# Attention scores from stacked high and low halves of q and k, and two more weight blocks split on GpSimd, in a two-layer hybrid encoder

## The chip, the cores and the metric

One core of a Trainium2 chip runs the whole program. The metric is device time in microseconds (us). Below, PE is the matrix engine (TensorE), PEld its weight loads, DVE the VectorE, ACT the ScalarE, POOL the GpSimd, SP the engine whose queue issues the DMAs.

## What is computed

Two layers over 256 positions of width 1024, in float32. Each layer is a half SwiGLU feed-forward, a mixer and another half feed-forward, each followed by a residual and a LayerNorm. The mixer's three branches are fed by one projection; the attention branch is what the change touches:

```
z = x @ w_in
sc_b, sc_c, sc_h, q, k, v, cc_a, cc_gate = split(z)
y_sc = sc_b * dwconv3(sc_c * sc_h)
q, k = rope(q), rope(k)                       # 8 query heads, 2 key heads, 64 wide
y_att = softmax(q k^T / 8, |i-j| <= 128, learned sink per head) @ v
u = dwconv31(cc_a * sigmoid(cc_gate)) + cc_conv_b
y_cc = silu(layer_norm(u))
mixer = concat(y_sc, y_att, y_cc) @ w_out
```

## The kernel before

Weights come as blocks of 128x2048 float32 (1 MB), 78 per layer: 33 for a feed-forward, 12 for the mixer, 33 again. `fetch` (L102) has SP load a block into one of five `raw` buffers. `emit_block` (L115) splits it with `split` (L95): ACT rounds it to a float32r part `hi` (L96), and a subtraction gives the rest `lo` (L97). The subtraction is DVE's, in one piece of 128x2048, except for the blocks of `POOL_BLOCKS` (L43): these go to POOL in four pieces of 128x512. `ON_POOL` (L42) names them by their number from the mixer's first block, 7 to 15 before the change. `use` (L135) hands a split block to the matmuls, `release` and `tick` (L140, L147) emit the next split when a block has been read; five `hi` and `lo` buffers exist. Each float32 product is then three matmuls: hi*hi, hi*lo, lo*hi (`mm3`, L152).

`mixer` (L476) is written out by hand in its order, and a scheduler of the language then sets the order on each engine. First come the projections for the gate of the long convolution (`ga`) and for q (blocks 0 to 3, `proj_n`), then k and v (block 4, `kv`), then three column projections `proj_c` (block 5 into `psc`, 6 into `psh`, 7 into `psb`). `glu` and `glu_turned` make `upad`, the long convolution's padded input; `emit_conv` (L541) lays its 31 taps for two channel groups, 62 instructions of 128x256 that DVE does between other work (`fill`, L143; tap lines L549, L551). `rotate` applies the rotary embedding on DVE (L500 to L503).

`q_turned` and `k_turned` (L517, L524) transpose the rotated q and k on PE (L205) and have ACT copy them from PSUM (L521, L527). `scores` (L560) does, for a pair of heads in two groups j, plain float32 matmuls of 64 rows (L566): group j lives on partitions 64j to 64j+63 in both operands:

```
hp = slice(j * HD, (j + 1) * HD)
nc.tensor.matmul(scs[j][:, c, :], qT[t][hp, 2 * i + c, :], kT[hp, :], start=True, stop=False)
```

A bfloat16 matmul adds the mask (L568). There are eight such units, four in a layer: `S_(0)` to `S_(3)`. Each is followed by maxima on DVE (L576), exponentials on ACT, transposes (`T_`) and the product with v (`V_`). `cc_norm` and `cc_out` take the finished convolution through a LayerNorm and swish into `y[3]` (a pair yhh, yhl: rounded part and rest). `w_out` (L752) multiplies y[0] to y[3] by the output blocks, t being the tile of 128 positions and h the half of the columns. `boundary` (L281) closes the mixer: for tile 0 it gathers (L225), takes statistics (L220), normalises (L239, L240) and transposes the result for the next feed-forward.

Of the kernel before, what the change touches and what calls it, by code (L numbers as in the profile page):

```python
# [8 lines left out]
F32 = mybir.dt.float32  # L9
F32R = mybir.dt.float32r  # L10
BF16 = mybir.dt.bfloat16
AF = mybir.ActivationFunctionType
ALU = mybir.AluOpType
# [3 lines left out]
P = 128  # L17
D = 1024
S = 256
# [5 lines left out]
HD = 64  # L25
# [13 lines left out]
PER_MIX = 12  # L39
NBLOCKS = DEPTH * (2 * PER_FFN + PER_MIX)  # L40
W_OUT = (1, 2, 0, 3)
ON_POOL = range(7, 16)  # L42
POOL_BLOCKS = [l * (2 * PER_FFN + PER_MIX) + PER_FFN + i for l in range(DEPTH) for i in ON_POOL]  # L43


@with_exitstack
def encoder(ctx: ExitStack, tc: tile.TileContext, head_in, xt_in, x_in, w_in, gb_in, small_in, rope_in, out):
    nc = tc.nc
# [9 lines left out]
    mx = pool("mx", 1)  # L58
# [144 lines left out]
    def transpose(ps, srcs):  # L203
        for i, a in enumerate(srcs):
            nc.tensor.transpose(ps[:, i * P:(i + 1) * P], a, ident)  # L205
# [270 lines left out]
    def mixer(l, norm):  # L476
# [11 lines left out]
        nc.gpsimd.memset(upad, 0.0)  # L488
        ppad = mx.tile([P, 2, S + 2], F32, tag="ppad", name="ppad")
        nc.gpsimd.memset(ppad, 0.0)  # L490
        kT = mx.tile([P, S], F32, tag="kT", name="kT")
        half = HD // 2
        chan = lambda a: a.rearrange("p (c n) -> p c n", c=2)

# [19 lines left out]
            transpose(pt, [u[:, 0:P], u[:, P:2 * P]])  # L514
            nc.scalar.copy(upad[:, :, PAD + t * P:PAD + (t + 1) * P], chan(pt[:, 0:2 * P]))

        def q_turned(r):  # L517
            pq = tmp_bank()
            transpose(pq, [r[:, c * P:(c + 1) * P] for c in range(4)])
            q = mx.tile([P, 4, P], F32, tag="qT", bufs=2, name="qT")  # L520
            nc.scalar.copy(q.rearrange("p c n -> p (c n)"), pq)  # L521
            return q

        def k_turned(t, r):  # L524
            pk = tmp_bank()
            transpose(pk, [r[:, 0:P]])
            nc.scalar.copy(kT[:, t * P:(t + 1) * P], pk[:, 0:P])  # L527

        def kv(t, w):
            ps = tmp_bank()  # L530
# [29 lines left out]
        def scores(t, i):  # L560
            mo = 1 - t
            scs = [chan(bank()) for _ in range(2)]
            for c in range(2):
                for j in range(2):
                    hp = slice(j * HD, (j + 1) * HD)
                    nc.tensor.matmul(scs[j][:, c, :], qT[t][hp, 2 * i + c, :], kT[hp, :], start=True, stop=False)  # L566
                for j in range(2):
                    nc.tensor.matmul(scs[j][:, c, mo * P:(mo + 1) * P], ident_b, mask[:, t, :], start=False, stop=True)  # L568
            return scs

# [80 lines left out]
        qT, vn, rk = [], [], []  # L651
        ga, q = bank(), bank()
# [6 lines left out]
        r0 = rotate(0, q, NH)  # L659
# [2 lines left out]
        glu_turned(0, u0)  # L662
        proj_n(ga, 1, wga[1], 1)
        u1 = glu(ga)
        qT.append(q_turned(r0))
        proj_n(q, 1, wq[0], 0)
        glu_turned(1, u1)
        cacc = emit_conv()
# [10 lines left out]
        wc = use(KC)  # L679
        fill(6)  # L680
        proj_c(psc, wc, 0)
        qT.append(q_turned(r1))
        k_turned(0, rk0)
        k_turned(1, rk1)
        prs, pTs = {}, {}

        def softmax(u, scs):
# [196 lines left out]
```

## Time and profile before

| | |
|---|---|
| median of 3 runs | 935.88 us (935.44 to 935.91) |
| the profiled execution | 933.17 us, of which the span is 931.4 us |
| granted TensorE clock | 0.998 |
| PE busy | 918.5 us, 99% |
| DVE busy | 644.5 us, 69% |
| ACT busy | 458.5 us, 49% |
| POOL busy | 118.0 us, 13% |
| DMA | 174.01 MB, mean 187 GB/s |

The span runs from the first to the last instruction of the profiled execution; the other runs carry no trace. Busy shares are over the whole span; the two mixers lie at 189 to 279 us and at 648 to 738 us. In a timeline the starts of successive matmuls give what each one costs, as their shown durations overlap.

### The profile page before, as it was taken

The numbers are of one execution on the slowest core, as the hardware profiler recorded it, in microseconds if no ns is written. First come the engines' busy times: TensorE is split into PE (matmuls) and PEld (weight loads), VectorE is DVE, ScalarE is ACT, GpSimd is POOL, SyncE is SP. The second block draws the span as 40 slices with busy tenths as digits, with TensorE's granted clock in tenths as the row PEclk, the third lists the DMA queues.
The fourth block names the chain that finished last, engine by engine and source line by source line (L and its number), as shares of the span: only waits on it lengthen the run. The fifth ranks groups of instructions, "written<-read, shape, count | busy, mean of one in ns | idle before, by whom it ended". The sixth has DMA issues, their size and how long they took to land.

```text
span 931.4 us, 12150 instructions
## 1 busy us (share of the span) xinstructions
PE 918.5 (99%) x4912; PEld 778.1 (84%) x4912; DVE 644.5 (69%) x815; ACT 458.5 (49%) x593; POOL 118.0 (13%) x108
## 2 busy tenths in 40 slices
PE   9999999999999999999999999999999999999996
PEld 6888888888778888888888888888887788888885
DVE  6966556789976766665777655667799866666545
ACT  6744544346744544445444444444466454444530
POOL 0010000008581000000000000000274700000000
PEclk9999999999999999999999999999999999999999
DMA  9966465536235655554456555553652365555301
GB/s 353 372 254 254 176 224 183 181 139 224 91 136 183 232 218 180 187 203 170 164 210 232 192 180 214 193 177 139 223 184 91 135 233 219 181 187 199 111 1 45
DMA packets 25976, 174.01 MB, mean 187 GB/s; under 512 B 2880, under 2 KB 3136, under 8 KB 5696
## 3 DMA queue, kind: packets, MB, share of 16 engines
q1 hardware_dynamic: 25920, 173.24, 51.5%
q8 instruction: 38, 0.62, 0.3%
q14 instruction: 18, 0.15, 0.0%
HBM read 172.18 MB, written 1.05 MB: 186 GB/s over the span
## 4 chain that ended last, share of the span: by engine, by line
PE 90%; DVE 6%; POOL 1%; DMA 1%; issue 0%; ACT 0%; SPq 0%; DVEq 0%; ACTq 0%
PE wide L170 28%; PE wide L174 15%; PE bank L153 9%; PE bank L154 9%; PE bank L155 9%; PE bank L181 4%; PE bank L185 4%; PE bank L182 4%; DVE tmp L551 2%; PE tmp L205 1%; PE bank L195 1%; POOL lo L97 1%; PE tmp L154 1%; PE tmp L153 1%; PE tmp L155 1%; DVE mxs L576 1%
## 5 line engine op out<-in xcount | busy, mean ns | idle before, releaser
L97 DVE TENSOR_TENSOR lo<-raw,hi 128x2048 fp32r<-128x2048 f32 (+2 forms) x175 | 317.1, 1826 | 211.0 <-ACT hi L96 210.8
L96 ACT CAST hi<-raw 128x2048 fp32r<-128x2048 f32 (+2 forms) x247 | 306.7, 1271 | 246.9 <-PE wide L170 154.2
L170 PE MATMUL wide<-xT,hi 128*128 128x512 f32 x1152 | 274.1, 390 | 0.0
L170 PEld LDWEIGHTS wide<-xT,hi 128*128 128x128 f32 x1152 | 213.9, 188 | 43.0
L174 PEld LDWEIGHTS wide<-xT,lo 128*128 128x128 f32 x1152 | 147.7, 191 | 5.6
L174 PE MATMUL wide<-xT,lo 128*128 128x256 f32 x1152 | 149.4, 283 | 0.0
L153 PE MATMUL bank<-hi,hh 128*128 128x512 f32 (+1 forms) x352 | 137.2, 390 | 0.0
L154 PE MATMUL bank<-lo,hh 128*128 128x512 f32 (+1 forms) x352 | 137.0, 389 | 0.0
L155 PE MATMUL bank<-hi,hl 128*128 128x512 f32 (+1 forms) x352 | 136.5, 388 | 0.0
L97 POOL TENSOR_TENSOR lo<-raw,hi 128x512 fp32r<-128x512 f32 x72 | 97.1, 1378 | 65.3 <-ACT hi L96 65.1
L234 POOL TENSOR_TENSOR rstd<-ve,mhalf 128x1 f32<-128x1 f32 x12 | 11.5, 958 | 672.6 <-DVE ve L233 672.6
L155 PEld LDWEIGHTS bank<-hi,hl 128*128 128x128 f32 x352 | 66.1, 188 | 13.9
L96 ACT CAST hh<-big 128x512 fp32r<-128x512 f32 x36 | 22.4, 622 | 110.6 <-DVE big L376 110.6
L153 PEld LDWEIGHTS bank<-hi,hh 128*128 128x128 f32 x352 | 66.2, 188 | 12.6
L154 PEld LDWEIGHTS bank<-lo,hh 128*128 128x128 f32 x352 | 66.3, 188 | 12.2
L181 PE MATMUL bank<-hi,xT 128*128 128x512 f32 x160 | 64.7, 404 | 0.0
L182 PE MATMUL bank<-lo,xT 128*128 128x512 f32 x160 | 62.5, 391 | 0.0
L384 DVE TENSOR_TENSOR big<-wide,big 128x512 f32<-128x512 f32 x72 | 49.3, 684 | 6.9 <-ACT big L383 6.9
L551 DVE SCALAR_TENSOR_TENSOR tmp<-upad,wc,tmp 128x256 f32<-128x256 f32 x116 | 49.8, 478 | 0.2
L383 ACT COPY big<-wide 128x512 f32<-128x512 f32 x72 | 42.3, 587 | 11.4 <-PE wide L174 11.1
L185 PE MATMUL bank<-hi,xT 128*128 128x512 f32 x160 | 43.2, 392 | 0.0
L97 DVE TENSOR_TENSOR hl<-big,hh 128x512 fp32r<-128x512 f32 x36 | 24.9, 692 | 24.0 <-ACT hh L96 24.0
(139 smaller groups left out, 890.5 us busy)
## 6 DMA issues: line engine op xcount, KB each, us to landing
raw<-in_w SPq DMA_DIRECT2D x152, 1024.0 KB, 4.8
gb<-in_gb SPq DMA_DIRECT2D x6, 1024.0 KB, 5.0
raw<-in_w SPq DMA_DIRECT2D x4, 512.0 KB, 7.1
head<-in_head SPq DMA_DIRECT2D x4, 384.0 KB, 4.3
raw<-in_w SPq DMA_DIRECT2D x4, 256.0 KB, 5.6
x<-in_x SPq DMA_DIRECT2D x2, 512.0 KB, 5.6
out<-x SPq DMA_DIRECT2D x4, 256.0 KB, 2.1
xraw<-in_xt SPq DMA_DIRECT2D x2, 256.0 KB, 5.2
```

Of the source, the lines that this page charges most:

```text
L96: nc.scalar.copy(hi, src)
L97: (eng or nc.vector).tensor_tensor(lo, src, hi.bitcast(F32), ALU.subtract)
L153: nc.tensor.matmul(ps, ah, bh, start=first, stop=False)
L154: nc.tensor.matmul(ps, ah, bl, start=False, stop=False)
L155: nc.tensor.matmul(ps, al, bh, start=False, stop=last)
L170: nc.tensor.matmul(ps[:, c], w[0][:, k, cs], xT[:, :, k], start=k == 0, stop=False)
L174: nc.tensor.matmul(ps[:, c, 0], w[1][:, k, cs], xT_h[:, k], start=False, stop=k == KC - 1)
L181: nc.tensor.matmul(ps, xT_h[:, kk, t, :], w[0][:, k, :], start=kk == 0, stop=False)
L182: nc.tensor.matmul(ps, xT_h[:, kk, t, :], w[1][:, k, :], start=False, stop=False)
L185: nc.tensor.matmul(ps, xT_l[:, kk, t, :], w[0][:, k, :], start=False, stop=kk == KC - 1)
L384: nc.vector.tensor_tensor(av, ps[:, :, 0], av, ALU.add)
L551: nc.vector.scalar_tensor_tensor(dst, upad[:, c, k:k + S], wc2[:, c, k:k + 1], part, op0=ALU.mult, op1=ALU.add)
```

## The change

`ON_POOL` becomes 5 to 15: POOL subtracts the low parts of the mixer's blocks 5 and 6, counted from 0, too, and ACT rounds them in four pieces. `q_turned` makes two operands of 128 rows for each tile: for group j, ACT's rounded q on the group's own 64 partitions and DVE's rest on the other 64. They lie in `y[2]` and `y[3]`, which get their results later. `k_turned` waits for both tiles and makes for each group the rounded k on both halves and the rest on both halves: four casts on ACT, four subtractions on DVE. `scores` then takes two float32r matmuls of 128 rows per head, and each head's mask directly after them.

```
--- before.py
+++ after.py
@@ -39,7 +39,7 @@
 PER_MIX = 12
 NBLOCKS = DEPTH * (2 * PER_FFN + PER_MIX)
 W_OUT = (1, 2, 0, 3)
-ON_POOL = range(7, 16)
+ON_POOL = range(5, 16)
 POOL_BLOCKS = [l * (2 * PER_FFN + PER_MIX) + PER_FFN + i for l in range(DEPTH) for i in ON_POOL]
 
 
@@ -488,7 +488,7 @@
         nc.gpsimd.memset(upad, 0.0)
         ppad = mx.tile([P, 2, S + 2], F32, tag="ppad", name="ppad")
         nc.gpsimd.memset(ppad, 0.0)
-        kT = mx.tile([P, S], F32, tag="kT", name="kT")
+        kT = mx.tile([P, 2, 2, S], F32R, tag="kT", name="kT")
         half = HD // 2
         chan = lambda a: a.rearrange("p (c n) -> p c n", c=2)
 
@@ -514,17 +514,30 @@
             transpose(pt, [u[:, 0:P], u[:, P:2 * P]])
             nc.scalar.copy(upad[:, :, PAD + t * P:PAD + (t + 1) * P], chan(pt[:, 0:2 * P]))
 
-        def q_turned(r):
+        def q_turned(t, r):
+
             pq = tmp_bank()
             transpose(pq, [r[:, c * P:(c + 1) * P] for c in range(4)])
-            q = mx.tile([P, 4, P], F32, tag="qT", bufs=2, name="qT")
-            nc.scalar.copy(q.rearrange("p c n -> p (c n)"), pq)
-            return q
-
-        def k_turned(t, r):
+            qs = [a.rearrange("p c n -> p (c n)") for a in y[2 + t]]
+            for j, q in enumerate(qs):
+                own, other = (slice(i * HD, (i + 1) * HD) for i in (j, 1 - j))
+                nc.scalar.copy(q[own], pq[own])
+                nc.vector.tensor_tensor(q[other], pq[own], q[own].bitcast(F32), ALU.subtract)
+            return [q.rearrange("p (c n) -> p c n", c=4) for q in qs]
+
+        def k_turned(rs):
+
             pk = tmp_bank()
-            transpose(pk, [r[:, 0:P]])
-            nc.scalar.copy(kT[:, t * P:(t + 1) * P], pk[:, 0:P])
+            transpose(pk, [r[:, 0:P] for r in rs])
+            for part in range(2):
+                for j in range(2):
+                    own = slice(j * HD, (j + 1) * HD)
+                    for half in range(2):
+                        to = slice(half * HD, (half + 1) * HD)
+                        if part == 0:
+                            nc.scalar.copy(kT[to, j, 0], pk[own, 0:S])
+                        else:
+                            nc.vector.tensor_tensor(kT[to, j, 1], pk[own, 0:S], kT[own, j, 0].bitcast(F32), ALU.subtract)
 
         def kv(t, w):
             ps = tmp_bank()
@@ -562,9 +575,8 @@
             scs = [chan(bank()) for _ in range(2)]
             for c in range(2):
                 for j in range(2):
-                    hp = slice(j * HD, (j + 1) * HD)
-                    nc.tensor.matmul(scs[j][:, c, :], qT[t][hp, 2 * i + c, :], kT[hp, :], start=True, stop=False)
-                for j in range(2):
+                    for part in range(2):
+                        nc.tensor.matmul(scs[j][:, c, :], qT[t][j][:, 2 * i + c, :], kT[:, j, part], start=part == 0, stop=False)
                     nc.tensor.matmul(scs[j][:, c, mo * P:(mo + 1) * P], ident_b, mask[:, t, :], start=False, stop=True)
             return scs
 
@@ -662,7 +674,7 @@
         glu_turned(0, u0)
         proj_n(ga, 1, wga[1], 1)
         u1 = glu(ga)
-        qT.append(q_turned(r0))
+        qT.append(q_turned(0, r0))
         proj_n(q, 1, wq[0], 0)
         glu_turned(1, u1)
         cacc = emit_conv()
@@ -679,9 +691,8 @@
         wc = use(KC)
         fill(6)
         proj_c(psc, wc, 0)
-        qT.append(q_turned(r1))
-        k_turned(0, rk0)
-        k_turned(1, rk1)
+        qT.append(q_turned(1, r1))
+        k_turned((rk0, rk1))
         prs, pTs = {}, {}
 
         def softmax(u, scs):
```

Line numbers from L524 on are larger in the changed kernel: its tap is L562 and L564, its score L579, its mask L580, its maximum L588.

**Where instructions move.** The first place is DVE's queue in the first mixer, from the rotation of tile 0's q to that of tile 1's. `lo_1731` and `lo_1760` are the low parts of blocks 5 and 6, `upad` the convolution's input.

```order
 L503 TENSOR_TENSOR big<-big 128x512
-L97 TENSOR_TENSOR lo_1731<-raw_1421,hi_1730 128x2048
 L509 SCALAR_TENSOR_TENSOR big<-big,bank 128x256
-L97 TENSOR_TENSOR lo_1760<-raw_1467,hi_1759 128x2048
-L549 TENSOR_SCALAR tmp<-upad,wc_1609,small 128x256
-L551 SCALAR_TENSOR_TENSOR tmp<-upad,wc_1609,tmp 128x256 x3
+L525 TENSOR_TENSOR yhh<-tmp,yhh 64x512
+L525 TENSOR_TENSOR yhl<-tmp,yhl 64x512
+L562 TENSOR_SCALAR tmp<-upad,wc_1609,small 128x256
+L564 SCALAR_TENSOR_TENSOR tmp<-upad,wc_1609,tmp 128x256 x3
 L500 TENSOR_TENSOR big<-bank,rope 128x512
```

The two large subtractions have left; two small ones for q stand ahead of the first tap.

The second place is DVE's queue after the last key rotation, up to the first unit's maxima. Before:

```order
L500 TENSOR_TENSOR big<-tmp,rope 128x128
L501 TENSOR_TENSOR big<-tmp,rope 128x2x32
L502 TENSOR_TENSOR big<-tmp,rope 128x2x32
L551 SCALAR_TENSOR_TENSOR tmp<-upad,wc_1609,tmp 128x256
L503 TENSOR_TENSOR big<-big 128x128
L551 SCALAR_TENSOR_TENSOR tmp<-upad,wc_1609,tmp 128x256 x12
L576 TENSOR_REDUCE mxs<-bank 128x2 x2
L551 SCALAR_TENSOR_TENSOR tmp<-upad,wc_1609,tmp 128x256
L577 SCALAR_TENSOR_TENSOR nm<-mxs,nsink 128x4
```

Now:

```order
L564 SCALAR_TENSOR_TENSOR tmp<-upad,wc_1609,tmp 128x256 x5
L525 TENSOR_TENSOR yhh<-tmp,yhh 64x512
L564 SCALAR_TENSOR_TENSOR tmp<-upad,wc_1609,tmp 128x256 x2
L525 TENSOR_TENSOR yhl<-tmp,yhl 64x512
L564 SCALAR_TENSOR_TENSOR tmp<-upad,wc_1609,tmp 128x256 x5
L540 TENSOR_TENSOR kT<-tmp,kT 64x256 x4
L588 TENSOR_REDUCE mxs<-bank 128x2
L564 SCALAR_TENSOR_TENSOR tmp<-upad,wc_1609,tmp 128x256
L588 TENSOR_REDUCE mxs<-bank 128x2
L564 SCALAR_TENSOR_TENSOR tmp<-upad,wc_1609,tmp 128x256
L589 SCALAR_TENSOR_TENSOR nm<-mxs,nsink 128x4
```

Two subtractions for q and four for k now stand between the taps, ahead of the first maxima, and no tap stands between the last of them and the first maximum.

The third place is the end of the mixer. On PE: `hi43` is an output block for y[1] (yhh_1620), `hi44` that for y[3] (yhh_1624, yhl_1625); banks 2316 and 2317 are tile 0's halves before, 2353 and 2354 now, 2456 is tile 1's first half. Before:

```order
L153 MATMUL bank_2317<-hi43_2032,yhh_1620 128x512
L154 MATMUL bank_2317<-lo43_2033,yhh_1620 128x512
L155 MATMUL bank_2317<-hi43_2032,yhl_1621 128x512
L153 MATMUL bank_2316<-hi44_2174,yhh_1624 128x512
L154 MATMUL bank_2316<-lo44_2175,yhh_1624 128x512
L155 MATMUL bank_2316<-hi44_2174,yhl_1625 128x512
L153 MATMUL bank_2316<-hi44_2174,yhh_1624 128x512
```

Now:

```order
L153 MATMUL bank_2456<-hi43_2057,yhh_1620 128x512
L154 MATMUL bank_2456<-lo43_2058,yhh_1620 128x512
L155 MATMUL bank_2456<-hi43_2057,yhl_1621 128x512
L153 MATMUL bank_2353<-hi44_2207,yhh_1624 128x512
L154 MATMUL bank_2353<-lo44_2208,yhh_1624 128x512
L153 MATMUL bank_2354<-hi44_2207,yhh_1624 128x512
L155 MATMUL bank_2353<-hi44_2207,yhl_1625 128x512
```

All of y[1]'s work for tile 0 has moved further ahead, and six matmuls for tile 1 now stand directly before the first use of y[3]. DVE's queue behind it, x_650 being tile 0 and x_652 tile 1:

```order
 L225 SCALAR_TENSOR_TENSOR x_650<-x_650,bank 128x512
 L220 BN_STATS sts<-x_650 128x6
-L232 BN_AGGR mv<-sts 128x2
+L225 SCALAR_TENSOR_TENSOR x_652<-x_652,bank 128x512
+L232 BN_AGGR mv<-sts 128x2
+L220 BN_STATS sts<-x_652 128x6
 L233 TENSOR_SCALAR ve<-mv 128x1
 L239 SCALAR_TENSOR_TENSOR x_650<-x_650,mv,gb 128x512 x2
 L240 SCALAR_TENSOR_TENSOR x_650<-x_650,rstd,gb 128x512 x2
 L225 SCALAR_TENSOR_TENSOR x_652<-x_652,bank 128x512
```

A gather and a statistics instruction of tile 1 now stand before tile 0's normalisation.

## Rows read from the trace of the kernel before

**Rows 1.** The page's first part: busy time, share of the span, instructions.
```profile
PE 918.5 (99%) x4912; PEld 778.1 (84%) x4912; DVE 644.5 (69%) x815; ACT 458.5 (49%) x593; POOL 118.0 (13%) x108
```

**Rows 2.** Windows of the first mixer: length, busy us of PE, PEld, DVE, ACT, POOL.
```profile
200.00:210.00 10.00, 10.00 (x51) 8.23 (x50) 5.82 (x8) 5.44 (x6) 0.00 (x0) 1.00 0.52 200
...
220.00:230.00 10.00, 10.00 (x81) 8.84 (x81) 9.68 (x26) 5.16 (x15) 8.56 (x7) 1.00 0.59 206
```

**Rows 3.** Timeline of DVE: start us, us, engine line op, idle before.
```profile
206.11 2.29 DVE L97 TENSOR_TENSOR lo<-raw,hi 128x2048 fp32r<-128x2048 f32 x1 [2.59 <-ACT hi L96]
...
209.36 2.29 DVE L97 TENSOR_TENSOR lo<-raw,hi 128x2048 fp32r<-128x2048 f32 x1 [0.62 <-ACT hi L96]
211.56 0.54 DVE L549 TENSOR_SCALAR tmp<-upad,wc,small 128x256 f32<-128x256 f32 x1
```

**Rows 4.** Timeline of PE and of ACT: transposes for upad, then its copy.
```profile
210.12 0.38 PE L205 MATMUL tmp<-ident,big 128*128 128x128 f32 x2
...
210.86 0.37 ACT L515 COPY upad<-tmp 128x256 f32<-128x256 f32 x1
```

**Rows 5.** Timeline of DVE: two subtractions that read PSUM, and what follows each.
```profile
202.24 0.68 DVE L97 TENSOR_TENSOR xT<-tmp,xT 128x512 fp32r<-128x512 f32 x1
202.83 0.68 DVE L503 TENSOR_TENSOR big<-big 128x512 f32<-128x512 f32 x1
...
248.43 0.41 DVE L97 TENSOR_TENSOR yhl<-tmp,yhh 128x256 fp32r<-128x256 f32 x1
248.76 0.68 DVE L604 COPY big<-bank 128x512 f32<-128x512 f32 x1
```

**Rows 6.** Timeline of POOL and of DVE: low parts, and small instructions beside them.
```profile
211.03 16.24 POOL L97 TENSOR_TENSOR lo<-raw,hi 128x512 fp32r<-128x512 f32 x12 [17.54 <-ACT hi L96]
...
217.34 1.20 DVE L503 TENSOR_TENSOR big<-big 128x128 f32<-128x128 f32 x1
...
220.88 0.28 DVE L503 TENSOR_TENSOR big<-big 128x128 f32<-128x128 f32 x1
...
228.25 1.14 DVE L578 TENSOR_TENSOR es<-small,nm 128x4 f32<-128x4 f32 x1
```

**Rows 7.** Timeline of PE around the first score unit.
```profile
224.23 0.28 PE L154 MATMUL tmp<-xT,hi 128*128 128x256 f32 x1
224.44 0.70 PE L566 MATMUL bank<-kT,qT 64*128 64x256 f32 x4
225.07 0.28 PE L568 MATMUL bank<-mask,ident_b 128*128 128x128 bf16 x2
...
226.02 0.36 PE L155 MATMUL tmp<-xT,lo 128*128 128x256 f32 x1
226.22 0.28 PE L153 MATMUL tmp<-xT,hi 128*128 128x256 f32 x1
...
226.34 0.28 PE L154 MATMUL tmp<-xT,hi 128*128 128x256 f32 x1
```

**Rows 8.** Timeline of DVE and PE: the last taps, y[3]'s rest, its first use.
```profile
256.53 0.86 DVE L551 SCALAR_TENSOR_TENSOR big<-upad,wc,tmp 128x256 f32<-128x256 f32 x2
...
267.07 1.01 DVE L97 TENSOR_TENSOR yhl<-big,yhh 128x512 fp32r<-128x512 f32 x1 [0.69 <-ACT yhh L96]
...
268.24 0.39 PE L153 MATMUL bank<-hi,yhh 128*128 128x512 f32 x1
...
726.65 1.01 DVE L97 TENSOR_TENSOR yhl<-big,yhh 128x512 fp32r<-128x512 f32 x1 [0.69 <-ACT yhh L96]
```

**Rows 9.** Timeline of PE and DVE: last use of y[3] for tile 0, to the next feed-forward.
```profile
270.73 0.39 PE L155 MATMUL bank<-hi,yhl 128*128 128x512 f32 x1
...
275.82 2.44 DVE L240 SCALAR_TENSOR_TENSOR x<-x,rstd,gb 128x512 f32<-128x512 f32 x2 [0.44 <-POOL rstd L234]
...
276.72 0.63 PE L205 MATMUL tmp<-ident,x 128*128 128x128 f32 x4 [0.84 <-DVE x L240]
...
278.79 0.47 PE L181 MATMUL bank<-hi,xT 128*128 128x512 f32 x1
```

## The prediction

> **What bounds the kernel now.** I read the page's first part before anything else: PE is busy for 99% of the span [rows 1]. In general, then, only what PE is spared, or what PE is made to wait for, can move the time. The change lies in the two mixers, so I read those stage by stage next, in windows and then in the timelines of single engines. The reader should see in the windows that a second engine is full there: DVE is busy 5.82 us of 10 before the convolution starts, and 9.68 of 10 once it runs [rows 2]. Two engines at their limit at once means that the mixer is a balance. The place where it shows is y[3], the convolution's result. Its last taps end at 256.53 + 0.86 = 257.39 us; LayerNorm and swish bring its rest to DVE's queue, and this is done at 267.07 + 1.01 = 268.08; PE comes for y[3] at 268.24 [rows 8]. So PE arrives 0.16 us after the data, and its third matmul there is the first to read the rest: some 0.6 us of slack. From there a fixed chain runs: tile 0's last matmul on y[3] starts at 270.73, gather, statistics and normalisation follow, its transposes start at 276.72 after PE has idled 0.84, and the next feed-forward starts at 278.79 [rows 9], which is 10.71 us after y[3]'s rest. The second layer has the same rest at 726.65 + 1.01 = 727.66 with the same 0.69 of waiting ahead of it [rows 8], so I work out one layer and take it twice. Whatever delays the end of the taps delays the feed-forward, once that slack is used up.
>
> **The change, part by part, for one layer.**
>
> The two large subtractions leave DVE: 2 x 2.2 us (each 2.29, the first tap starting 2.2 after the second). But they stand where DVE was waiting: 2.59 us idle ahead of the first, 0.62 ahead of the second, both for ACT [rows 3]. What follows them, the first tap at 211.56, needs the second tile's half of `upad`. PE transposes that at 210.12 to 210.50, and ACT copies it at 210.86 to 211.23 [rows 4]. With ACT free the first tap could start about 0.7 earlier (210.50 + 0.37 = 210.87 against 211.56). In the changed order ACT has two q casts to do ahead of that copy, which take what was free. I take 0, with ends of -0.7 and +0.5.
>
> The new subtractions go onto DVE. For tile 0 the two of 64x512 stand ahead of the first tap, in idle time: nothing. For tile 1 two of 64x512, and four of 64x256 for k, stand among the taps, where DVE has no idle time. DVE's time goes by the free size, as the nearest rows have it: a subtraction from PSUM with 512 per partition holds DVE for 202.83 - 202.24 = 0.59, one with 256 for 248.76 - 248.43 = 0.33 [rows 5]. That is 2 x 0.59 + 4 x 0.33 = **+2.5 us**. The order shows that 24 of the 62 taps stand ahead of the first maximum both before and now, so nothing behind this is lightened in return.
>
> New waits on DVE. The subtraction for q's tile 1 waits for ACT's cast behind its transposes, and the first maximum waits for the first score unit, which can now only begin when the last k rests are being written; no tap stands between. A whole unit takes 226.22 - 224.23 less two steps of 0.12, or 1.75 us, on PE [rows 7], which bounds that wait; ACT's cast of 512 per partition bounds the other by twice the 0.37 of 256 [rows 4], 0.74. Between 0 and 2.5 I take 0.8: the scheduler has laid the first matmuls of the unit earlier, as soon as its first operands exist.
>
> POOL gets 8 more pieces at 16.24 / 12 = 1.35 us, or 10.8 us [rows 6]. It can start by 206.11, when DVE now takes block 5's [rows 3], against 211.03, and has done both by about 217. The products around the first score unit at 224 are block 5's [rows 7]; 38 of them stand ahead of it in the order, so they begin near 219, and block 6's come after them: as a term by itself, nothing. POOL's later blocks are pushed back by some 5 us; the next, 7, then ends near 222, and its products come after all of block 6's. What the extra work does is fill POOL's gaps among the softmaxes. Small DVE instructions with both inputs in SBUF are sometimes held there: one 128x128 addition took 1.20 us and its twin 0.28, both beside POOL's work, and a 128x4 addition took 1.14 [rows 6]. About five more such instructions will meet POOL at work. If none is held, it costs 0; if each is held for 0.9, 4.5 us; and instructions held today may escape, for -1.5. The two rows with the same shape say half of them; but one that is held only shifts the next one's place against POOL's pieces. I take +0.2, nearest to the row that is not held, and keep -1.5 and +4.5. The Trainium skill (SBUF — State Buffer, Who interferes with whom) says that a DVE instruction with two SBUF inputs is fully blocked by a GpSimd instruction that started first and reads SBUF. The 1.14 row agrees with it, the 0.28 row, beside POOL's pieces too, does not; by the rule alone this term would be about +3.4, half a piece for each of five, and the layer's sum +6.7 instead of +3.5.
>
> PE. A pair of score products of 64 rows, run beside each other, takes 225.07 - 224.44 = 0.63 now; four float32r products take 4 x 0.12 = 0.48. With 8 pairs a layer that spares 1.2 us. Two more entries into a mask per unit, each with 0.20 - 0.12 = 0.08 behind it [rows 7], take 0.6 back, and transposes that the new order breaks into single ones about as much again. PE is spared between 0 and 1.2 us, but as it then waits for y[3], none of it counts.
>
> The tail. Twelve matmuls for y[1] now stand ahead of the convolution's transposes, which is where PE would otherwise wait for the later taps, and six for tile 1 stand ahead of y[3]. Nine matmuls and a drain, 2.2 us at 0.23, run from y[3]'s rest to tile 0's last product. Then 276.72 - 271.12 = 5.6 us to the transposes as now [rows 9], 1.3 for a gather and a statistics instruction that stand inside the chain now, half of 2.44 for the second half's normalisation and 0.4 for its transposes, behind which no product waits any more: 2.2 + 5.6 + 1.3 + 1.2 + 0.4 = 10.7 us to the feed-forward, against 10.71. The slack is gone with the order: the rest of y[3] now releases nine of the twelve products. I take 0, with ends of -1 (POOL no longer holds the normalisation: its two halves take 2.44 us [rows 9]) and +1.
>
> **Sum.** 0 + 2.5 + 0.8 + 0.2 + 0 = +3.5 us a layer, +7.0 for two. Against the profiled execution: 933.17 + 7.0 = 940.2 us. That execution lies 2.7 us below the median of the runs, 935.88, which is what the result is held against: 935.9 + 7.0 = **942.9 us**.
>
> **Rivals.**
>
> *PE's saving counts (faster).* If DVE absorbs the 2.5 us, the end of the taps stays, and PE keeps what the scores spare. It decides where y[3]'s rest is ready by the time PE comes: the taps must end by about 257.4 plus PE's own new delay there. Price: 2.4 us for 16 pairs, some of the saved weight on the merged k transposes, less masks: about -2.5, so 933.4 us. For it: PE's 99% [rows 1]. Against: no idle DVE time among the taps [rows 2].
>
> *Only the order costs.* The taps end in time, but six matmuls (6 x 0.23 = 1.4 us) have moved from behind y[3] to ahead of it, and no longer cover the normalisation chain. Behind tile 0's last product, 8.5 us stand instead of 278.79 - 271.12 = 7.7. 1.4 + 0.8 less 0.9 spared gives +1.3 a layer: 938.5 us. It needs DVE to lose nothing that PE sees.
>
> *POOL holds DVE up.* Each of the five further small instructions is held for half a piece on average, 5 x 1.35 / 2 = +3.4 in place of +0.2: +6.7 a layer, 949.3 us. For it: the two held rows; against: the third [rows 6].
>
> *Nothing is spared and nothing lost.* The taps end in time, and the four float32r products of a pair, with their masks, cost what the pair costs today, 0.63 or 0.16 each instead of 0.12 [rows 7]: 935.9 us. The Trainium skill (FP8 and Floating Point Precision, TensorE Precision Notes) says that a true float32 product takes four passes through the array; by that rule the pair of today, its halves beside each other, is four passes of 256 columns, as many as the four products now, and PE is spared nothing. The trace's 0.63 against 0.48 speaks against that.
>
> **How the numbers follow.** The measurement of this kernel tells changes of over 0.2% (1.9 us) from none. My forecast, DVE's added work delaying y[3] in both layers, gets 0.60, with a range of its own of 939 to 947. The order alone gets 0.12, POOL 0.10, nothing spared 0.07, PE's saving 0.11. The first three are slower: 0.82. Same 0.07, faster 0.11. For a range of 8 in 10, I go down to 936.5 (a layer at +0.3) and up to 948 (a layer at +6), which leaves out the fast rival, some of the unchanged one and the upper half of POOL's case.
>
> **What would show it.** Right: in the changed profile the last taps end 3 to 4 us later in the stage than now (about 260.9), y[3]'s rest about 271.6, the feed-forward's first product about 282.3; PE shows idle time for y[3] or the normalisation of over 1 us, where it has 0.84 now; the first tap still starts near 211.5, with DVE idle ahead of it. Wrong: taps that end by 258, small DVE instructions with a clearly different mean, or a step of the new scores that is not near 0.12. Then the sum is wrong at that term. POOL's last pieces of blocks 5 to 9 should end near 232 with no one waiting for them.

## The result, and the profile after

| | before | changed |
|---|---|---|
| median, same chip | 935.66 us (935.25 to 935.91, 4 runs) | 949.66 us (949.32 to 950.20, 4 runs) |
| profiled execution | 933.17 us | 949.32 us |
| its span, granted clock | 931.4 us, 0.998 | 947.5 us, 0.991 |

The changed kernel takes 1.0153 times as long, with a 95% interval of 1.0139 to 1.0166: it is 14.0 us slower. The forecast was 942.9 us, with a range up to 948.0. Its direction came true, its size was half of what came.

The page's first part answers to [rows 1]. PE's share has fallen from 99 to 97%, so PE now waits somewhere:

```profile
PE 923.5 (97%) x4912; PEld 784.5 (83%) x4912; DVE 648.0 (68%) x827; ACT 463.9 (49%) x613; POOL 136.6 (14%) x124
```

DVE's timeline in the first mixer (start us, us, engine, line, operation, idle before), from the first tap to the normalisation:

```profile
212.35 0.55 DVE L562 TENSOR_SCALAR tmp<-upad,wc,small 128x256 f32<-128x256 f32 x1 [0.88 <-ACT upad L515]
...
224.47 0.68 DVE L525 TENSOR_TENSOR yhh<-tmp,yhh 64x512 fp32r<-64x512 f32 x1
...
225.97 0.69 DVE L525 TENSOR_TENSOR yhl<-tmp,yhl 64x512 fp32r<-64x512 f32 x1
...
228.81 1.75 DVE L540 TENSOR_TENSOR kT<-tmp,kT 64x256 fp32r<-64x256 f32 x4
230.87 0.69 DVE L588 TENSOR_REDUCE mxs<-bank 128x2 f32<-128x512 f32 x1 [0.32 <-PE bank L580]
...
262.27 0.86 DVE L564 SCALAR_TENSOR_TENSOR big<-upad,wc,tmp 128x256 f32<-128x256 f32 x2
...
273.13 1.02 DVE L97 TENSOR_TENSOR yhl<-big,yhh 128x512 fp32r<-128x512 f32 x1 [0.69 <-ACT yhh L96]
275.43 0.69 DVE L225 SCALAR_TENSOR_TENSOR x<-x,bank 128x512 f32<-128x512 f32 x1 [1.29 <-PE bank L155]
...
279.45 2.22 DVE L239 SCALAR_TENSOR_TENSOR x<-x,mv,gb 128x512 f32<-128x512 f32 x2
281.60 3.43 DVE L240 SCALAR_TENSOR_TENSOR x<-x,rstd,gb 128x512 f32<-128x512 f32 x2
```

The taps end at 263.13 [rows 8: 257.39], y[3]'s rest at 274.15 [rows 8: 268.08]. PE's timeline at the mixer's end answers to [rows 9]:

```profile
280.23 0.39 PE L155 MATMUL bank<-hi,yhl 128*128 128x512 f32 x1
283.41 0.66 PE L205 MATMUL tmp<-ident,x 128*128 128x128 f32 x4 [2.79 <-DVE x L240]
285.08 0.66 PE L205 MATMUL tmp<-ident,x 128*128 128x128 f32 x4 [1.02 <-DVE x L240]
285.49 0.67 PE L181 MATMUL bank<-hi,xT 128*128 128x512 f32 x1
285.96 0.63 PE L182 MATMUL bank<-lo,xT 128*128 128x512 f32 x1
286.39 0.63 PE L181 MATMUL bank<-hi,xT 128*128 128x512 f32 x1
...
289.92 0.39 PE L181 MATMUL bank<-hi,xT 128*128 128x512 f32 x1
290.15 0.39 PE L182 MATMUL bank<-lo,xT 128*128 128x512 f32 x1
```

PE idles 2.79 and 1.02 us where it idled 0.84 and 0.36, and the feed-forward's first product comes at 285.49 instead of 278.79. Then something new shows: the starts of the feed-forward's first products lie 0.43 us apart (285.96 to 286.39), and from 289.92 on 0.23. The windows of the changed kernel (length, busy us of PE, PEld, DVE, ACT, POOL, then the granted clock) show the clock beside it:

```profile
280.00:290.00 10.00, 6.20 (x24) 4.58 (x23) 10.00 (x14) 4.77 (x9) 8.54 (x7) 0.83 0.41 123
...
750.00:760.00 10.00, 9.26 (x32) 7.39 (x33) 9.86 (x16) 2.21 (x4) 5.62 (x4) 0.67 0.45 175
```

The granted clock is at 0.83 and 0.67 in the mean of the stretch behind each mixer, in which PE spends part of the time at the lower of its two levels (1.2 and 2.4 GHz), after it had idled. In the trace of before both stretches have 1.00. The Trainium skill (TensorE: Matmul & The Clock Gate, The HAM clock gate) names these two levels and says that the lower one is the default, and that activity releases it; the steps of 0.43 and 0.23 us agree with it.

### The profile page after: what moved, and what is told of

Its sections match the earlier page's. It is cut to its first block, busy times and chain, and to the rows that moved or that the text cites. A ratio compares the mean times of both kernels' runs of the same rounds, so it can differ in the third digit from the quotient of the medians.

```text
span 947.5 us, 12188 instructions
## 1 busy us (share of the span) xinstructions
PE 923.5 (97%) x4912; PEld 784.5 (83%) x4912; DVE 648.0 (68%) x827; ACT 463.9 (49%) x613; POOL 136.6 (14%) x124
## 4 chain that ended last, share of the span: by engine, by line
PE 89%; DVE 8%; ACT 1%; DMA 1%; issue 1%; DVEq 0%; ACTq 0%
PE wide L170 28%; PE wide L174 15%; PE bank L153 9%; PE bank L155 9%; PE bank L154 9%; PE bank L181 4%; PE bank L182 4%; PE bank L185 4%; DVE tmp L564 2%; PE tmp L205 1%; PE bank L205 1%; PE bank L195 1%; PE tmp L626 1%; PE bank L579 1%; DVE sts L220 1%
## 5 line engine op out<-in xcount | busy, mean ns | idle before, releaser
L97 DVE TENSOR_TENSOR lo<-raw,hi 128x2048 fp32r<-128x2048 f32 (+2 forms) x171 | 308.9, 1820 | 205.8 <-ACT hi L96 205.6
L96 ACT CAST hi<-raw 128x512 fp32r<-128x512 f32 (+2 forms) x259 | 307.5, 1219 | 233.2 <-PE wide L170 154.0
L97 POOL TENSOR_TENSOR lo<-raw,hi 128x512 fp32r<-128x512 f32 x88 | 115.8, 1350 | 44.4 <-ACT hi L96 44.4
L181 PE MATMUL bank<-hi,xT 128*128 128x512 f32 x160 | 66.6, 416 | 0.0
L182 PE MATMUL bank<-lo,xT 128*128 128x512 f32 x160 | 64.4, 403 | 0.0
L564 DVE SCALAR_TENSOR_TENSOR tmp<-upad,wc,tmp 128x256 f32<-128x256 f32 x116 | 49.8, 477 | 0.3
L383 ACT COPY big<-wide 128x512 f32<-128x512 f32 x72 | 42.3, 587 | 12.4 <-PE wide L174 12.1
L185 PE MATMUL bank<-hi,xT 128*128 128x512 f32 x160 | 43.2, 392 | 0.0
```

Source lines behind the costliest of these rows:

```text
L96: nc.scalar.copy(hi, src)
L97: (eng or nc.vector).tensor_tensor(lo, src, hi.bitcast(F32), ALU.subtract)
L181: nc.tensor.matmul(ps, xT_h[:, kk, t, :], w[0][:, k, :], start=kk == 0, stop=False)
L182: nc.tensor.matmul(ps, xT_h[:, kk, t, :], w[1][:, k, :], start=False, stop=False)
L185: nc.tensor.matmul(ps, xT_l[:, kk, t, :], w[0][:, k, :], start=False, stop=kk == KC - 1)
L564: nc.vector.scalar_tensor_tensor(dst, upad[:, c, k:k + S], wc2[:, c, k:k + 1], part, op0=ALU.mult, op1=ALU.add)
```

## The experiments

In all of them layer and stage are read as above. The prediction's account in one line: DVE's work among the taps delays y[3]. The rivals: POOL's holds on DVE, or the new order of the output products.

**A second trace of before.** No edit.

> The kernel before, unchanged, for a second trace of it. Its first trace lies 2.5 us below the median. Theory A: the difference is spread over the span or lies outside the mixers, and the taps end again 45.8 us after the first tap. Rival: in a usual execution the mixers are some 1.2 us longer each than in the first trace, because small DVE instructions meet POOL's pieces otherwise; then the taps take about 47 us, and what the change costs a layer is that much less.

It took 935.72 us. The rival holds. These are DVE's windows from first tap to last, of this trace and then of the changed kernel:

```profile
212.01:259.01 47.00, 46.70 (x332) 38.16 (x331) 46.78 (x114) 32.00 (x89) 31.85 (x26) 1.00 0.40 144
```

```profile
212.35:263.13 50.78, 47.70 (x345) 41.48 (x344) 49.56 (x120) 34.09 (x92) 34.47 (x29) 1.00 0.46 164
```

The taps take 47.00 us, not 45.83, and 47.07 in the run with `ON_POOL` alone below. The first trace of before was a short execution, and the second is the fair one to compare with. By it, with the start of the mixers put level, the changed kernel is late by:

| place | layer 1 | layer 2 |
|---|---|---|
| first tap | +0.2 | +0.2 |
| first maximum | +3.4 | +3.4 |
| last tap's end | +4.0 | +4.0 |
| y[3]'s rest | +4.3 | +4.3 |
| first transposes of the normalised tile | +4.9 | +5.2 |
| next transposes in the feed-forward, some 12 us on | +6.3 | +7.2 |

With 0.15 us from the start of the program this makes the 13.6 us between the two spans (933.9 and 947.5). The same two windows show PE: it is idle for 0.30 us among the taps before (47.00 less 46.70), and for 3.08 in the changed kernel.

**One part at a time.** `ON_POOL` alone in the kernel before, and the scores alone:

```
-ON_POOL = range(7, 16)
+ON_POOL = range(5, 16)
```

> The kernel before, with blocks 5 and 6 given to POOL and nothing else. Theory A (the taps on DVE set the end, and POOL's extra pieces hold small DVE instructions for 0.85 us a layer): the taps end 0 to 0.9 us later in each layer, of which PE sees what exceeds some 0.6 of slack; 936 to 937.5 us. Theory B (POOL's extra work is a main cause, holding DVE among the taps and at the normalisation): +1.9 us a layer, about 939.5. If the freed DVE time before the first tap counted, about 934.5.

```
-ON_POOL = range(5, 16)
+ON_POOL = range(7, 16)
```

> The changed kernel with POOL's blocks as before (7 to 15). Theory A: the subtractions for q and k among the taps are the main cost and stay; only the 0.85 us a layer that POOL holds DVE goes, and two subtractions of 2.29 us come back ahead of the first tap, into idle time: 947 to 949 us. Theory B (POOL): 944 to 946 us.

The first took 935.64 us, ratio 1.0000 (0.9991 to 1.0009): POOL's two blocks alone cost nothing and gain nothing. The scores alone took 951.42 us (ratio 1.0155 to 1.0185), a little more than the whole change, though the two intervals overlap; neither theory had that. The loss belongs to the scores.

**POOL silent.** In both kernels, for blocks 5 to 15 (`ON_POOL` is set to them in the kernel before, too), the low part is left out:

```
-        lo = wpool.tile([P, BLK], F32R, tag="lo", name=f"lo{i}")
+        lo = hi if i in POOL_BLOCKS else wpool.tile([P, BLK], F32R, tag="lo", name=f"lo{i}")
...
-            split(hi[:, cs], lo[:, cs], raw[:, cs], nc.gpsimd if i in POOL_BLOCKS else None)
+            if i in POOL_BLOCKS:
+                nc.scalar.copy(hi[:, cs], raw[:, cs])
+            else:
+                split(hi[:, cs], lo[:, cs], raw[:, cs])
```

> The kernel before with POOL silent in the mixer: of blocks 5 to 15 the low part is not computed, and the rounded part stands in its place. In the trace of before, small DVE instructions among the taps take 4.4 us a layer more than their shortest, and the two halves of the normalisation 1.0. Theory A: PE is the limit, so only PE's idle time at the end (1.2 us a layer) can come back: 933 to 935 us. Rival (DVE sets the end before too): up to 5 us a layer, 926.

> The changed kernel with POOL silent in the mixer in the same way. Theory A (the change costs because DVE is full, and what fills it is the rests, about 3 us, on top of 5.3 us a layer that POOL holds small DVE instructions): without POOL's holds the taps end about where they did before, the normalisation is 2 us shorter, PE does not idle and its clock stays: 934 to 937 us. Rival (the rests, their handovers and the new order cost 5 us a layer whatever POOL does): 944 to 947 us.

Before came to 928.42 us, changed to 934.46. So the scores cost 6.0 us with POOL silent, and 14.0 with POOL at work. Theory A had the sum for the changed kernel, but expected too little of the kernel before: POOL's subtractions cost 7.3 us there, though PE is at 99%. The windows of the taps, before and then changed:

```profile
211.56:255.86 44.30, 44.30 (x329) 36.66 (x327) 41.56 (x113) 31.65 (x89) 0.73 (x2) 1.00 0.40 144
```

```profile
212.02:260.44 48.42, 47.89 (x347) 41.65 (x345) 44.62 (x120) 33.68 (x92) 0.73 (x2) 1.00 0.41 153
```

DVE's busy time tells the terms apart. With POOL silent it differs by 44.62 - 41.56 = 3.06 us: the rests. With POOL at work it is 46.78 - 41.56 = 5.2 us more in the kernel before, and 49.56 - 44.62 = 4.9 us more in the changed one: the holds, nearly the same in both. DVE's idle time is 0.2 us before and 1.2 changed (window less busy): the waits.

**A dose.** In the kernel before, five copies from PSUM that nobody reads, for q's tile 1:

```
+            for i in range(extra):
+                nc.vector.tensor_copy(y[2 + i % 2][i // 2 % 2].rearrange("p c n -> p (c n)"), pq)
...
-        qT.append(q_turned(r1))
+        qT.append(q_turned(r1, 5))
```

> The kernel before with five copies of 128x512 (0.6 us each) that nobody reads, on DVE, at the place where the changed kernel takes the rests of q's tile 1: 3.0 us a layer among the taps ahead of the first maximum. Theory A (DVE's work there delays the taps' end one for one, and PE waits): the taps take 3 us more than in the second trace of before (47.0), and the time is 5 to 6.5 us above before, 940.5 to 942; more, if PE then idles long enough ahead of the transposes for the clock to fall. Rival (the mixer is bound by PE's own stalls, and 3 us of DVE are hidden): 935 to 937.

944.41 us, 8.85 above before: over theory A's 5 to 6.5, with the fall of the clock that it named. Scores, masks and POOL's blocks are those of before. DVE and PE in its first mixer:

```profile
271.50 1.02 DVE L97 TENSOR_TENSOR yhl<-big,yhh 128x512 fp32r<-128x512 f32 x1 [0.69 <-ACT yhh L96]
...
280.27 3.42 DVE L240 SCALAR_TENSOR_TENSOR x<-x,rstd,gb 128x512 f32<-128x512 f32 x2 [0.44 <-POOL rstd L234]
```

```profile
282.07 1.11 PE L205 MATMUL tmp<-ident,x 128*128 128x128 f32 x4 [2.40 <-DVE x L240]
...
283.41 0.63 PE L154 MATMUL bank<-lo,yhh 128*128 128x512 f32 x1
283.84 0.63 PE L155 MATMUL bank<-hi,yhl 128*128 128x512 f32 x1
```

The 3.0 us delay the last tap by 2.35 (the taps take 49.35 us) and y[3]'s rest by 2.9 (272.52 against 269.68, with 0.08 at the start), nearly one for one. Behind it the same thing happens as in the changed kernel: the transposes are 3.8 us late, PE has idled 2.40, and the products directly behind go in steps of 0.43. In the second layer PE idles 2.25 us, the granted clock stays at 1.00 in the stretch behind, and the transposes alone are 4.2 late. A layer loses 4.6 and 4.2 us for 3.0 of work. The amplification is thus a property of the mixer's end, not of the new scores.

**Less work on DVE.** The rests left out (the products then read the rounded parts), and another form with fewer of them:

```
-                nc.vector.tensor_tensor(q[other], pq[own], q[own].bitcast(F32), ALU.subtract)
...
-                            nc.vector.tensor_tensor(kT[to, j, 1], pk[own, 0:S], kT[own, j, 0].bitcast(F32), ALU.subtract)
```

> The changed kernel without the rests of q and k: no subtraction on DVE for them, and the two products of a head are taken from the rounded halves (64 rows each), so the low parts are left out of the scores. Casts, masks and POOL's blocks stay. Theory A (the rests and their handovers are some 4 us a layer): the taps take about 47 instead of 50.8 us, and with PE's idle time at the end the clock's part goes too: 938 to 942 us. Rival (POOL's holds and the new order are the larger part): 945 or more.

```
+            split(*qs, pq)
...
+            split(kT[:, 0], kT[:, 1], pk[:, 0:S])
...
+                for n, (a, b) in enumerate(((0, 0), (0, 1), (1, 0))):
+                    for j in range(2):
+                        hp = slice(j * HD, (j + 1) * HD)
+                        nc.tensor.matmul(scs[j][:, c, :], qT[t][a][hp, 2 * i + c, :], kT[hp, b, :], start=n == 0, stop=False)
```

> The changed kernel with another form of the scores: q and k split on their own partitions into rounded part and rest (one cast and one subtraction of 128x512 for each q tile, one of 128x256 for k), and three float32r products of 64 rows for each head. Theory A (DVE's work among the taps sets the end): 0.6 + 0.33 = 0.9 us of subtractions there instead of 3.0, and the handovers between ACT and DVE gone, 2.1 to 2.7 us a layer less: 944 to 945.5 us, less still where PE's idle time at the end falls and the clock stays. Rival (the order of the output products and POOL cost it): 948 to 950 us. PE: a unit of 12 such products at 0.12 each would take 1.5 us, less if the two groups run beside each other.

Both miss theory A: 947.93 and 947.50 us, only 1.7 and 2.2 less. The first lies in its rival's range, the second between its two. Their windows of the taps, in this order:

```profile
211.37:261.74 50.37, 49.68 (x342) 41.72 (x341) 48.07 (x114) 34.07 (x92) 35.07 (x29) 1.00 0.45 159
```

```profile
211.52:262.31 50.79, 48.03 (x358) 40.54 (x357) 50.12 (x116) 32.13 (x88) 35.51 (x29) 1.00 0.45 161
```

Without the rests DVE's busy time should fall by 3.06 from 49.56; it falls by 1.5, and DVE waits 2.3 us instead of 1.2. With the three products it does not fall at all. What is taken away comes back, as holds and as waits: in the three-product kernel the rotation's 128x512 addition takes 1.72 us (0.68 unheld), and one 128x4 addition 1.00 (0.15). The holds are the same in both layers of a kernel, but differ between kernels: 4.9 us in the changed one, 48.07 - 41.56 = 6.5 without the rests. I read from this that they depend on where each small instruction falls against POOL's pieces, and that any new order deals them anew; no run tests that by itself. So the dose shows that 3 us more on DVE are enough for such a loss, but not that the rests are what the changed kernel loses by: without them 12.4 us of the 14.0 stay (947.93 against 935.56 in the same session). Which part of the new scores, the rests, the handovers or the new order, costs the 4 us at the taps while POOL works stays open.

**The clock and the end.** Unread products where PE idles, in the changed kernel:

```
...
+                for _ in range((6, 2)[h]):
+                    nc.tensor.matmul(pt[0:12, 0:S], self.sts[0][:, 0:2].rearrange("p a b -> p (a b)"), warm, start=True, stop=True)
```

> The changed kernel with products that nobody reads (6 and 2 of float32 with 256 columns) put on PE where it idles 2.8 and 1.0 us ahead of the mixer's last transposes. Theory A (PE's idle time there lets the granted clock fall, and the next eight products take 0.43 us each instead of 0.23): the clock stays at 1.00 in the slice behind, the products take 0.23, and 1.3 and 1.6 us come back: about 946.8 us. Rival (the clock falls for another reason, or the products behind wait for their data anyway): 949.7, or up to 951 where the added products delay the transposes.

946.42 us, 3.2 less, as theory A has it. Its PE and its windows:

```profile
285.35 0.47 PE L181 MATMUL bank<-hi,xT 128*128 128x512 f32 x1
285.67 0.39 PE L182 MATMUL bank<-lo,xT 128*128 128x512 f32 x1
285.90 0.40 PE L181 MATMUL bank<-hi,xT 128*128 128x512 f32 x1
```

```profile
280.00:290.00 10.00, 9.23 (x44) 6.08 (x43) 10.00 (x14) 4.07 (x8) 7.44 (x6) 1.00 0.52 179
...
750.00:760.00 10.00, 10.00 (x49) 7.96 (x48) 8.86 (x15) 2.90 (x6) 3.52 (x3) 1.00 0.43 143
```

The clock stays at 1.00 in both stretches, and the steps are 0.23 us. So the last 1.3 and 2.0 us of the table are the clock's. From the first transposes to the next ones this run takes 10.96 and 10.93 us, the changed kernel 11.96 and 12.64, before 10.61 and 10.65: 1.0 and 1.7 come back here, while the added products take some time themselves. Another 0.7 us between the two traces lies ahead of the first tap (211.61 for 212.35) and has nothing to do with the edit. PE's idle time does not bring the fall each time: after 2.25 us in the dose's second layer, and after 2.69 in that of the three-product form, the stretch behind has 1.00. The next run takes POOL away from the normalisation:

```
-ON_POOL = range(5, 16)
+ON_POOL = range(5, 12)
```

> The changed kernel with POOL taking blocks 5 to 11 only; blocks 12 to 15, the first four of the next feed-forward, go to DVE in pieces of 128x2048. Theory A (POOL beside the normalisation holds its two halves, 3.43 us instead of 1.41; PE then idles 2.8 us and the clock falls): the halves take 1.4 us, the transposes come 2 us earlier a layer, and the clock stays at 1.00: 943 to 946 us. Rival (the new order of the output products makes PE idle, whatever POOL does): 948 to 950. If DVE's four blocks of 2.29 us stand ahead of the normalisation or come late for the feed-forward: 952 or more.

951.61 us. Theory A's first half came: each pair of halves takes 1.41 us. But two of DVE's own blocks now stand ahead of y[3]'s rest, which is ready only at 276.86, and others ahead of the gathers; PE idles 4.33 us, and the steps of 0.43 are there again. This run does not tell POOL's share at the end apart.

**Ways around it.** POOL's subtractions in pieces of 128x256:

```
...
+                for c in range(cs.start, cs.stop, n // 2):
+                    s = slice(c, c + n // 2)
+                    nc.gpsimd.tensor_tensor(lo[:, s], raw[:, s], hi[:, s].bitcast(F32), ALU.subtract)
```

> The kernel before, with POOL's subtractions in pieces of 128x256 instead of 128x512. Theory A (a held DVE instruction waits for the rest of the piece that POOL is in; with POOL silent 7.3 us went): the holds halve, 2 to 3.5 us less, 932 to 934. Rival (DVE waits for POOL's work as such, whatever its pieces): 935.5 to 936; if shorter pieces cost POOL more in all and the blocks come late: 937 or more.

> The changed kernel, with POOL's subtractions in pieces of 128x256. Theory A: the holds among the taps and at the normalisation (3.43 us for its two halves) shorten by about half, PE idles less ahead of the last transposes, and with it the clock may stay: 942 to 946 us. Rival (the rests and the order cost it all): 949.5.

936.36 us for before (ratio 0.9999 to 1.0017), and 981.42 for the changed kernel. In the kernel before the taps do shorten, to 45.11 us, and y[3]'s rest comes 2.5 us sooner (267.20). But the normalisation also needs `rstd`, which POOL computes, in its queue behind its pieces. `rstd` does not come sooner with them, and DVE waits for it longer than the 0.44 us of the second trace of before:

```profile
276.35 2.34 DVE L246 SCALAR_TENSOR_TENSOR x<-x,rstd,gb 128x512 f32<-128x512 f32 x2 [1.82 <-POOL rstd L240]
```

The reason for the 981.42 stands below, under the hardware. Then the copies of the turned probabilities:

```
-                if j == 0:
-                    nc.scalar.copy(pT, pp)
-                else:
-                    nc.vector.tensor_copy(pT, pp)
+                nc.scalar.copy(pT, pp)
```

> The kernel before with all copies of the turned probabilities on ACT (four of 0.68 us a layer leave DVE). Theory A (DVE's load among the taps sets the mixer's time before, too): up to 2.7 us a layer less, 930 to 933 us. Rival (PE is the limit before): 934.5 to 936.

> The kernel before with POOL's pieces of 128x256 and all copies of the turned probabilities on ACT. Theory A: DVE is relieved by 2.7 us a layer and by half of its holds; with POOL silent 928.4 was reached, so 929 to 933 us. Rival (ACT holds up the exponentials, or PE is the limit): 935 or more.

In the kernel before this gives 935.37 us (ratio 0.9994 to 1.0012), and 934.40 with the shorter pieces too (0.9984 to 1.0005). The taps end 2 us earlier (256.92 for 259.01), but y[3]'s rest comes when it did (269.54 for 269.68): without the change something other than the taps sets it, and PE now waits 1.0 us in each layer for ACT's copies. The same four copies in the three-product form, once with the unread products and once with the shorter pieces:

> The changed kernel with the three products of 64 rows, the same four copies on ACT, and the unread products of 256 columns where PE idles ahead of the last transposes. Theory A: the three-product kernel is at 947.5; 2.7 us a layer leave DVE, and the clock's 1.3 to 2.0 us a layer come back: 938 to 941 us. Rival (POOL's holds move to other instructions, so that little is won among the taps): 944 or more.

> The changed kernel with the three products of 64 rows, POOL's pieces of 128x256, and all copies of the turned probabilities on ACT (four of 0.68 us a layer leave DVE). Theory A (DVE's load among the taps sets the end): DVE has 2.7 us less than in the three-product kernel at 947.5 and half of its holds, so that it stands as in the kernel before or better: 932 to 937 us. Rival (ACT then holds up the exponentials): 940 or more.

941.84 us, just above theory A's range, is the best of the changed forms, and still above before. The other came to 970.07, for the same reason as the 981.42. Two more on the kernel before, the sum of sink and maximum on POOL, and the four copies on ACT with POOL's blocks cut to 7 to 11:

```
-            nc.vector.tensor_tensor(es, sink[:, hs], nm, ALU.add)
+            nc.gpsimd.tensor_tensor(es, sink[:, hs], nm, ALU.add)
```

> The kernel before with the sum of sink and maximum (128x4, four a layer, 3.1 us of DVE in all, most of it held) given to POOL. Theory A (PE is the limit before): 0 to 1 us a layer less, 934 to 936 us. Rival (DVE's taps set the end in a usual execution): 2 us a layer less, 932; if the exponentials then wait for POOL, 937 or more.

```
-ON_POOL = range(7, 16)
+ON_POOL = range(7, 12)
```

> The kernel before with the four copies on ACT and POOL taking blocks 7 to 11 only. Theory A: among the taps 2.7 us a layer less, at the normalisation 1.0 less: 928.5 to 932 us. Rival (DVE's four blocks of 2.29 us near the end of the mixer delay the gathers or the feed-forward): 936 or more.

Both lost: 939.54 and 942.42 us. In the second the two halves of the normalisation take 1.41 us, as expected, but y[3]'s rest comes 3.2 us later (272.90), where DVE now does blocks 12 to 15 itself. No version that computes the whole result measurably beats the kernel before.

## Why the prediction was half right

Point by point, in a layer, against the second trace of before:

- **The two large subtractions: 0.** Right: the first tap is 0.2 us late.
- **The new subtractions: +2.5.** 3.06 by DVE's busy time with POOL silent. The four for k take 1.75 us together, 0.44 from one to the next, where I took 0.33 from a subtraction with the same 256 per partition.
- **New waits on DVE: +0.8.** DVE's idle time among the taps went from 0.2 to 1.2: +1.0. Two waits I did not see were on other engines: the second q cast stands 1.62 us on ACT until DVE's first subtraction, which reads the same bank, is done, and PE idles 1.00 ahead of the k transposes.

```profile
225.19 0.58 ACT L524 CAST yhl<-tmp 64x512 fp32r<-64x512 f32 x1 [1.62 <-DVE yhh L525]
```

```profile
226.81 0.41 PE L205 MATMUL tmp<-ident,big 128*128 128x128 f32 x2 [1.00 <-DVE yhl L525]
```

- **POOL holding small instructions: +0.2.** -0.3 (4.9 for 5.2). The rival that priced this at +3.4 is wrong for the difference, and POOL's two more blocks alone cost nothing (935.64 us). That its 949.3 lies beside the measured 949.66 is chance. What POOL costs either kernel is larger than I read: 7.3 us in the kernel before.
- **PE spared, none of it counting.** Right: a head's two products take 0.24 us and its mask 0.04, so the products of two heads take 0.48, where a pair of the old ones took 0.63 [rows 7], and the time is not gained.

```profile
232.15 0.40 PE L579 MATMUL bank<-kT,yhh 128*128 128x256 f32 x2
232.39 0.23 PE L580 MATMUL bank<-mask,ident_b 128*128 128x128 bf16 x1
232.43 0.48 PE L579 MATMUL bank<-kT,yhl 128*128 128x256 f32 x2
```

- Sum at the last tap: +3.5 forecast, +4.0 measured. This part stood in its size. Its path was not all mine: PE has lost 2.8 us by waits among the taps already (3.08 for 0.30), where I had it wait at y[3].
- **The tail: 0, ends -1 to +1.** This is the first of two steps that failed. From the last tap to the normalised tile's transposes a layer loses 1.0 to 1.2 us more: 0.35 on the way to y[3]'s rest, 0.9 behind it in the second mixer and 0.6 in the first (9.26 us from y[3]'s rest to the transposes, for 278.32 - 269.68 = 8.64). That alone lies at the end of its range. The second trace of before has these lines there, of DVE and of PE:

```profile
271.41 0.69 DVE L225 SCALAR_TENSOR_TENSOR x<-x,bank 128x512 f32<-128x512 f32 x1 [1.73 <-PE bank L155]
...
274.53 2.45 DVE L239 SCALAR_TENSOR_TENSOR x<-x,mv,gb 128x512 f32<-128x512 f32 x2
277.42 2.44 DVE L240 SCALAR_TENSOR_TENSOR x<-x,rstd,gb 128x512 f32<-128x512 f32 x2 [0.44 <-POOL rstd L234]
```

```profile
278.32 0.63 PE L205 MATMUL tmp<-ident,x 128*128 128x128 f32 x4 [0.83 <-DVE x L240]
```

In the first mixer the new order brings the first gather 0.45 us closer to y[3]'s rest (1.28 us, not 1.73); tile 1's gather and statistics make the way from there to the normalisation 0.90 longer (4.02, not 3.12); from there to the transposes it is 0.17 longer (3.96, not 3.79). The end of -1, that POOL no longer holds the normalisation, did not come: its two pairs of halves take 2.22 and 3.43 us, where they took 2.45 and 2.44. I had also read the chain as DVE's alone, though my own row says that it waits for POOL's `rstd` [rows 9]. The new order is not needed for a long tail: in the dose and in the three-product form no instruction of tile 1 stands ahead of the normalisation, and the way from y[3]'s rest to the transposes still takes 9.55 and 9.56 us. In the changed kernel with POOL silent it takes 7.42, order and all: the 1.8 us between that and 9.26 are POOL's.

- **The clock: no term.** This is the second step that failed, and the larger. I wrote that PE would show over 1 us of idle time for the normalisation, and gave that time no price beyond itself. PE idled 2.79 us, and the products behind ran in part at the lower level: +1.3 and +2.0 us, which is 3.3 of the 14.0. The run with the unread products had 1.0 and 1.7 of it back.

So the missing 7.0 us are, over two layers: 0.9 at the taps, 2.2 between the last tap and the transposes, 3.3 for the clock, and 0.6 that the two traces do not place. What I read the slack and the taps from mattered as well: the first trace was 2.5 us shorter than the second, and nearly all of that lay in the two mixers' taps.

## What to carry to other kernels

When a change makes PE wait where it did not, price the wait twice: for itself, and for the products behind it if the granted clock then falls; filling the wait with products that nobody reads shows which part is the clock's. Where a second engine is full, work added to it may cost nearly one for one at the next thing PE needs (2.9 us for 3.0 here), but work taken from it may return next to nothing, as its place is filled by holds and waits of others. Take a second trace of the kernel before, when its profiled execution lies off the median by as much as the terms that are to be read from it.

## What the runs showed of the hardware

DVE can be held far longer than one of POOL's pieces. In the changed kernel with pieces of 128x256, this is DVE, and then POOL, in the first mixer:

```profile
215.77 17.58 DVE L509 TENSOR_TENSOR big<-big 128x512 f32<-128x512 f32 x1
```

```profile
205.14 27.66 POOL L134 TENSOR_TENSOR lo<-raw,hi 128x256 fp32r<-128x256 f32 x40 [11.37 <-ACT hi L131]
```

An addition that takes 0.68 us unheld took 17.58: it ended 0.55 us after POOL's run of forty pieces did (232.80), some 25 pieces of 27.66 / 40 = 0.69 us later than it began. PE idled 15.44 us behind it in each layer, which is the 31 us of that run. With pieces of 128x512 POOL also works without a break, and the same addition gets through within about one piece:

```profile
205.46 30.59 POOL L97 TENSOR_TENSOR lo<-raw,hi 128x512 fp32r<-128x512 f32 x24 [11.37 <-ACT hi L96]
```

```profile
216.09 1.26 DVE L503 TENSOR_TENSOR big<-big 128x512 f32<-128x512 f32 x1
```

The Trainium skill (SBUF — State Buffer, Who interferes with whom) says that DVE's second SBUF input comes through the read interface that it shares with GpSimd, that the shared pair is an exclusive lock, and that the order of issue decides who blocks. The 1.26 us agree with that; the 17.58 go beyond it, as some 25 of POOL's pieces began and ended while the addition stood there.

Short pieces alone do not do this. In the kernel before with the same pieces, the same addition stands inside a run of twenty-six of them, and gets through in 0.99 us:

```profile
215.10 0.99 DVE L509 TENSOR_TENSOR big<-big 128x512 f32<-128x512 f32 x1
```

```profile
210.84 19.18 POOL L134 TENSOR_TENSOR lo<-raw,hi 128x256 fp32r<-128x256 f32 x26 [17.54 <-ACT hi L131]
```

There a piece of POOL's that begins 0.40 us behind it takes 1.19 us, where its neighbours take 0.74: POOL waits for once. What decides between the two cases stays open.
